# A decoder layer with its order and engines written in two tables: both tables drawn up anew

## The chip, the cores and the metric

One core of a Trainium2 chip runs the whole layer. The metric is the device time of one execution in microseconds (us); several runs of the same kernel give a median. The profile is of one further execution, taken by the hardware profiler. Engines are named as in the profile: PE (TensorE, matrix multiply) with PEld (its weight loads), DVE (VectorE), ACT (ScalarE), POOL (GpSimd), SP (SyncE, which issues nearly all transfers).

## What is computed

The reference is one layer of a hybrid decoder with 512 tokens and model width 1024, all in float32. Cut to what matters:

```python
def reference(x, c, ...):                       # x (1, 512, 1024), c (1, 1024)
    mod = silu(c) @ ada_w + ada_b               # 6 vectors of 1024: shift, scale, gate, twice
    sh1, sc1, g1, sh2, sc2, g2 = split(mod, 6)
    h = rms_norm(x, pre_norm_mix) * (1 + sc1) + sh1
    y = hybrid_mixer(h, ...)
    x = x + (1 + g1) * rms_norm(y, post_norm_mix)
    h = rms_norm(x, pre_norm_mlp) * (1 + sc2) + sh2
    y = square(relu(h @ w_ff1)) @ w_ff2         # 1024 -> 4096 -> 1024
    return x + (1 + g2) * rms_norm(y, post_norm_mlp)

def hybrid_mixer(h, ...):
    g_rnn, x_rnn, q, k_c, v_c, k_s, v_s, k_w, v_w, gate_logits = split(h @ w_in, ...)
    rnn = gelu(g_rnn) * rg_lru(causal_conv4(x_rnn))     # gated linear recurrence, width 512
    att = nsa_attention(...)     # 8 heads of 64; compressed + selected + window keys, ALiBi
    return concat(rms_norm(rnn), rms_norm(att)) @ w_out
```

## The kernel before

**Precision.** PE takes float32 numbers as a rounded high part and a low part, so most products are three matmuls: `mm3` issues high x high, high x low and low x high. Every operand has therefore to be split: a copy to the high part (`clk.copy`, on ACT or DVE) and a subtraction for the low part (`either("tensor_sub", ...)`, on DVE or POOL).

**Stages.** (1) The four token tiles of x are loaded and normalised (`XN`), transposed (`TR`) and modulated; ada weights give the shift and scale columns (`SU`). A first wave of matmuls (`MW`) makes six 512-column products at once in six PSUM banks while the weight tiles a0 to a7 arrive. (2) `AW` takes the wave out of PSUM: q to the tiles Q, keys to K1 and K2, and k_c and v_c to the tile kk, from which eight additions make the blocks `blk` of the compression. (3) `PR` runs the other projections in the order of the list ORDER: c00 to c13 (compression), x0 to x3 (recurrence input), q0 and q1, v, the recurrence's gates, g0 to g3. Later it runs the output projection (weight tiles o000 to o111). `VW` is the recurrence: conv, gates, scan, gelu. (4) `AS` makes the attention scores and their exponentials for 16 units, takes 1/denominator (`den`) and scales the tiles `p` by it; `AV` transposes the tiles p (PSUM tag tp), splits them into two tiles `pt` and multiplies by V (PSUM tag pv); `FA` finishes a token tile. (5) `RS` is the residual and norm, `TH` the transposes for the feed-forward part, `UF` the first four slices of the up projection. (6) `UP` is the up projection, one slice f0 to f31 of 128 columns at a time; `DA` is a first pass of the down projection over combinations of two slices (tiles ft, fs); `DN` is the second pass and the end: squares, norm, gate, residual and eight output transfers. `WL` loads the weight tiles (ring raw of four, SP's queue), `WS` splits them into hi_ and lo_ tiles. `AD` and `G2` make the other ada vectors out of tiles ar.

PSUM has eight banks, two for each of the tags f, s, pv and tp; whoever wants the next bank of a tag waits until the one before the last is read out.

**What sets the order.** The Python code calls the operations in some order, but during the recording nothing is issued: `put` appends each operation as a node, with the engines that could run it. At the end `flush` issues all nodes in the order of the table `PLAN`: 4836 nodes, two characters each, read as a number in base 90 with the digits of `ALPHA`. Where an operation could run on more than one engine (the copies of `clk.copy`, the operations of `either`, the choices of `clk.choose`), the table `PLACE` has one letter for it, by stream and in the order of recording: a for ACT, d for DVE, p for POOL. Each engine runs its own operations in the order of the table and waits by semaphores for the operands and the banks. The costs that stand in `act_way`, `elem_way` and `mm` order the recording only; the tables are drawn up elsewhere, by a planner that works with durations of its own.

```python
(way,) = self.nodes[ALPHA.index(a) * len(ALPHA) + ALPHA.index(b)].ways
way[2]()
...
mine = PLACE.get(self.name, "")[k:k + 1] if PLACE is not None else "adp"
ways = [w for w in ways if w[0][0] in (usual if mine in ("", ".") else mine)]
```

In the profile nearly every operation carries the line of the helper that issued it: L396 matmul, L400 transpose, L407 ACT, L441 DVE or POOL, L483 transfers. The tiles' names tell the operations apart; numbers in the names are left out (`hi_f` is the high part of some f slice, `r` a tile of the ring r8, `h` one of the h tiles).

Of the kernel before, what the change touches and what calls it, by code (L numbers as in the profile page):

```python
# [15 lines left out]
P = 128  # L16
S = 512
D = 1024
# [77 lines left out]
    '2d372E2K2~2G3S2c2j2g2e2f382b2l2i333V3T2k39352r2h2n342/2m2q363W2*2p3X2%2o2-3*3!3U2,3x3#2<2]3c3Y2?2=3y3C3Z'
    '3I3$2:3a2{2@583d2^3O3F3D3z3b3%3e3h3&3J3n3+3P3(3L3i3o3,3R3)3t4#3k3/4H3?3u4%3:3q4F3{3@45463w3A473G3M484M2.'
    '3|3f4O494C3l3r4A3<4N4B3-4g3=4G4$4h4i4k4l4m4j4Q4^4&4n4P4+4o4,4-4]GY4(4.2+2>4~4S5L504)2;514*3]5K4/2[4_3~4{'
    '4d2_3^5Y3E413K3Q52425D3B5X5M4|4}59533H3j445E5h5A5B5C435F5H5G3N5g5J3p3v5O3g3m5I5N5S3;5$3[5P3s4b7%5T3.5R3>'
    '4a3_3}4J5Q5#5Z5U5V5a5b5i5j5k4I5-5W5l5m5d5n5o5p5q5,5r4X5s7&4V5t5u4K5e627)6;4c6-5v4L5w6<6.6/5x6=5y615z5f6d'  # L100
    '5!5%6>6e4W6f7>6N674U6_6M5c6:7(68696@6A7?6V6B6{6?6C4e4R6D5_6E5&4Z4T6g6F4Y6G6H6I6U5(5)6[6J6|7+6K4f6q6}6L7|'
    '6h6O5*6p6P6i5+6]6^816Q6~6R6j6y5.5/6S6x6T6W5:726k5{716l6X6m6n5;5<7a6Y5=5>6a5?7b5@5[6Z5]73706o7c5^5}5|6r5~'
    '6c607C636s7B646t7R6u656v6w6b667N746z6!7S7D6#6$6%8L7z757T6&7@7!766(7[7o7]7}6)7~80777*7#788279836*847A7s85'
    '7t7p6+7q86877M88897r8A8B7w7u8V8W7vGW8Z8C8D8X7x7E8b7^8K8d937F8Y947,8E7-977_7.GZ957G997H7y7I9&7/8e4E7J8j9('
    '7K8k9)7L9+7O8h8F9,7P8f6,8G8O8i9E8P8QGa987Q7U9A9F7V8R9I7W9K7X9J9G7Y8M8S7Z8g7$7d8T7:7e8c9:7fG@9H8^8_9L8{9;'
    '7g8a9<7h7i968U8|8l8}7j8~9MAO8mG]90919*929B7;8u8q8v7kAP9=AU8w9N8x7l8y8r8z8!8#9l8$G^8%8&8(8)8*8n8+G_7m9C8o'
    '8,8t8-G[9m8.9T7<8p9D8N9V7=8s8/9O8:8H8;8<8=AV8>8I9W9n8?9r9o9s9X8@9Y9Z9aAS8[9b9R9c9p9d9t9e9v9f9w9x9q9y9g9U'
    'A59z8J9h9!AQAW9#ARA67{9$9iA79%AE9SAvB.A88]7nApAF9-AGAHAq9u9.AXA9B/AwAI9/9>AT9?9@Ar9[At9]9j9^9PAAAJAgCbAB'
    'CcAY9_C9AxAK9{AD9|9}9~AZ9QCdAdAcCiA.CAA/AuA0AhAzA!CNCjCkHPA>CpCqAsA#AfA?CrA:AeA@AiC#A<A$C$A%ALC%AaAjAbAM'
    'C+A&C,COA1C-A=BDBEANC/AyBHB5C:BJC;A[BFC<A(A;AkBtBIA]A2BGACA)BKHQBLA*AlA3B6BuB1BMA+B2BRB3C=A^BPC_A_BNC>A,'  # L110
# [1699 lines left out]
```

## Time and profile before

| | |
|---|---|
| median of three runs | 629.02 us (627.72 to 629.98) |
| the profiled execution, its own time | 627.82 us |
| its span, first to last instruction | 626.0 us, 9043 instructions |
| PE busy | 596.3 us (95%), 3060 matmuls and transposes |
| DVE busy | 539.2 us (86%) |
| ACT busy | 346.1 us (55%) |
| POOL busy | 209.1 us (33%) |
| moved by DMA | 102.15 MB, mean 163 GB/s |
| chain that ended last | PE 73%, DVE 11%, DMA 6%, ACT 5%, issue 3% |

A busy PE is not PE at its peak, since matmuls overlap; where matmuls follow one another without a wait, PE counts as busy throughout. A number in brackets behind a row of the timeline is the time for which the engine had been idle before it, and after the arrow stands what released it. The kernel's stages run one into the other: the wave ends at about 64 us, attention and recurrence lie between 98 and 269, the feed-forward part from 276 on.

### The profile page before, as it was taken

To read this page: it belongs to the slowest core of one execution; us is meant where nothing else is said; L and a number is where in the kernel's file an instruction comes from. 1 tells how busy PE (TensorE), PEld (TensorE's weight loads), DVE (VectorE), ACT (ScalarE), POOL (GpSimd) and SP (SyncE) were. 2 spreads that over 40 slices of the span, in tenths; PEclk is the share of its full clock that TensorE was granted. 3 is DMA by queue.
4 is the path that set the end of the run, shared out by engine and by line. 5 is a ranking of instruction groups with operands and counts; after the bars stand their busy time and mean duration, and the time that the engine had idled before them with its cause. 6 is when DMAs were issued, how large, how long until landed. Compare 5 with 4: busy or idle time off the path is not lost.

```text
span 626.0 us, 9043 instructions
## 1 busy us (share of the span) xinstructions
PE 596.3 (95%) x3060; PEld 497.9 (80%) x3060; DVE 539.2 (86%) x1072; ACT 346.1 (55%) x696; POOL 209.1 (33%) x209
## 2 busy tenths in 40 slices
PE   7999999998999999989999999999999999999992
PEld 6888788966777898869887888888887888878881
DVE  5986988979999988988888968787688789999897
ACT  6654525698999999687251220322322247465563
POOL 5001301652663175453204547641351231000113
PEclk9999999999999999999999999999999999999997
DMA  8968895430503302015664334254544426756613
GB/s 351 416 250 318 320 299 191 131 136 1 202 2 129 141 2 102 1 35 176 229 222 168 115 133 137 101 169 157 180 135 147 155 69 204 238 179 202 198 56 134
DMA packets 29430, 102.15 MB, mean 163 GB/s; under 512 B 3268, under 2 KB 3524, under 8 KB 29384
## 3 DMA queue, kind: packets, MB, share of 16 engines
q1 hardware_dynamic: 29240, 101.50, 46.4%
q8 instruction: 24, 0.39, 0.3%
q14 instruction: 22, 0.18, 0.1%
q10 hardware_dynamic: 144, 0.07, 0.0%
HBM read 99.47 MB, written 2.10 MB: 162 GB/s over the span
## 4 chain that ended last, share of the span: by engine, by line
PE 73%; DVE 11%; DMA 6%; ACT 5%; issue 3%; DVEq 0%; SPq 0%; ACTq 0%
PE f L396 36%; PE s L396 14%; PE pv L396 13%; PE tp L396 7%; DMA ar<-in_ada_t 4%; PE tp L400 4%; DVE r L441 3%; ACT p L407 2%; DVE fT L441 2%; ACT r L407 2%; DVE ar L441 1%; DMA raw_A11l<-in_wd 1%; DMA raw_A10l<-in_wd 1%; DVE p L441 1%; DMA r<-in_x 1%
## 5 line engine op out<-in xcount | busy, mean ns | idle before, releaser
L396 PE MATMUL f<-h,hi_f 128*128 128x512 f32 x224 | 87.7, 392 | 0.0
L396 PE MATMUL f<-h,lo_f 128*128 128x512 f32 x224 | 87.2, 389 | 0.0
L396 PE MATMUL f<-h2l,hi_f 128*128 128x512 f32 x224 | 87.2, 389 | 0.0
L407 ACT ACTIVATE fT<-f 128x512 f32<-128x512 f32 x30 | 17.8, 594 | 71.2 <-PE f L396 71.2
L396 PEld LDWEIGHTS f<-h,hi_f 128*128 128x128 f32 x224 | 42.1, 188 | 8.8 <-issue 0.2
L396 PEld LDWEIGHTS f<-h2l,hi_f 128*128 128x128 f32 x224 | 42.0, 188 | 8.6
L396 PEld LDWEIGHTS f<-h,lo_f 128*128 128x128 f32 x224 | 42.0, 188 | 8.5
L396 PE MATMUL f<-hi_o,h 128*128 128x512 f32 x128 | 47.7, 414 | 0.0
L407 ACT ACTIVATE p<-p,mx 128x32 f32<-128x32 f32 (+4 forms) x96 | 45.1, 472 | 3.8 <-DVE mx L441 3.6
L441 DVE TENSOR_TENSOR lo_f<-raw_f,hi_f 128x1024 fp32r<-128x1024 f32 x29 | 40.1, 1383 | 6.9 <-ACT hi_f L407 6.6
L400 PE MATMUL tp<-ident,p 128*128 128x128 f32 x192 | 41.6, 273 | 1.9 <-DVE pt L441 0.9
L396 PE MATMUL pv<-pt,V 128*128 128x256 f32 x160 | 42.2, 316 | 1.1 <-ACT pt L407 0.7
L441 POOL TENSOR_SCALAR p<-p,den 128x32 f32<-128x32 f32 (+4 forms) x43 | 35.7, 863 | 18.5 <-DVE den L441 15.5
L396 PE MATMUL s<-K,Q 128*128 128x288 f32 (+4 forms) x128 | 38.4, 336 | 0.5 <-DVE Q L441 0.3
L441 DVE TENSOR_TENSOR pt<-tp,pt 128x512 fp32r<-128x512 f32 (+1 forms) x56 | 33.6, 609 | 3.3 <-ACT pt L407 1.9
L407 ACT ACTIVATE hi_f<-raw_f 128x1024 fp32r<-128x1024 f32 x24 | 24.9, 1056 | 18.7 <-PE f L396 13.0
L396 PEld LDWEIGHTS pv<-pt,V 128*128 128x128 f32 x160 | 27.8, 189 | 6.1 <-DVE pt L441 2.1
L396 PE MATMUL s<-r,fs 128*128 128x512 f32 x96 | 32.5, 389 | 0.0
L396 PE MATMUL pv<-r,fs 128*128 128x512 f32 x96 | 31.8, 391 | 0.4 <-DVE r L441 0.4
L400 PEld LDWEIGHTS tp<-ident,p 128*128 128x128 f32 x192 | 25.0, 140 | 7.8 <-issue 1.8
L396 PE MATMUL tp<-r,fs 128*128 128x512 f32 x96 | 30.6, 389 | 0.0
L441 DVE CUSTOM_DVE_ANT_0 ar<-ar,silb 128x1024 f32<-128x1024 f32 x16 | 21.6, 1352 | 6.4 <-DMA ar<-in_ada_t 6.4
(732 smaller groups left out, 1817.0 us busy)
## 6 DMA issues: line engine op xcount, KB each, us to landing
raw_f<-in_wf SPq DMA_DIRECT2D x32, 512.0 KB, 3.5
...
```

The source lines that it names most:

```text
L396: lambda: self.nc.tensor.matmul(out, lhs, rhs, start=start, stop=stop))
L400: self.issue("pe", 0.109, [out], [src], lambda: self.nc.tensor.transpose(out, src, ident))
L407: return "act", cost, lambda: self.nc.scalar.activation(out, src, func, scale=scale, bias=bias, **kw), func
L441: return eng, cost, lambda: fn(out, *args, **kw), None
```

## The change

The operations, their operands and their dependences stay as they are. Both tables are replaced: `PLAN`, the order of all 4836 operations, and `PLACE`, the engine of those that have a choice. The planner was run with corrected durations for evacuations (reading PSUM out), transfers and GpSimd. The order of the streams and of the items in ORDER is untouched, and so are tile sizes, buffer counts and semaphores' rules.

```diff
 PLACE = {
-    '': 'dd',
...
-    'AV': 'dadaadddddaddddaaddadaaaaaaaaadaaaadaaaadaaaadaaaadaaaad',
-    'AW': 'adadaaddpppddpdp',
...
-    'TH': 'daddaadpddddaadddddddappddpddadd',
-    'UP': 'ddddddpdpddddpddpdddddddpddddddd',
-    'VW': 'pppdddpddppdppppppp',
...
-    'XN': 'aaaaaadaaaaa',
+    '': 'ad',
...
+    'AV': 'adddadddddaddddaaadadaaaaaaaaadadaadaaaadadaaaaaaadaaaad',
+    'AW': 'adaaaaaapdppdddd',
...
+    'TH': 'daddaaddddddaadddddpdaddadpdaadd',
+    'UP': 'ddpdddpddpddddddddpppdddddpddddd',
+    'VW': 'pdpdddpddppdppppppp',
...
+    'XN': 'paadaaaddaaa',
 }
 
 PLAN = (
-    '000O0P020Q0106400R0S0T0U0V0M074p4q084r0a0W0y040b4sGX4t090c030&0d0X0A554u0C4v054w0e4x0(0-4y0Y0H0N4z4!0D4:'
...
+    '000O0P020Q030R010S4E400T0U0V074p4q08090a0y0W0A0M0H0C0z0&0I0X0N0J0b4r0-4s0c0Y0B0(4t4u0D0)4v4w0d4x4y0=4z0Z'
...
 )
```

In PLACE 206 letters differ; the streams not shown with changes are AS (scalings of p and small products), DA, DN, FA and WS.

More of the change, by code (lines that the diff above doesn't have):

```diff
@@ L96 @@
[L96 to L110, printed above, removed]
@@ L181 @@
[L181 to L183 removed]
+    '000O0P020Q030R010S4E400T0U0V074p4q08090a0y0W0A0M0H0C0z0&0I0X0N0J0b4r0-4s0c0Y0B0(4t4u0D0)4v4w0d4x4y0=4z0Z'
+    '0E0.0*0e4!0!4:4;0f4<554=0>060^4>0/4?0F4@4[0g0G0h4D0i0;0_0:540?0|0{0}0j1O0#0~0K0kGX0]0L101E110l560@1P1C0m'
@@ new lines @@
+    '0+0n1F0o0[121j140,130p160%0q1k1G15181v170r19041l1H1A0s571B1D0<0t1J0u1M1=0v1I0w1N0x1K1R1Q1X1V1m0$1L1b1n1T'
+    '1U1>1o1]1p1q1W1r1a1s1^051S1w1c1_1t1{1Z1Y1?1e2M1x1|1h1g1@1$201z1[1i1u1f2X2Q1!2N2L1)1+1}1(1.1d1#2Y2&1;2R1y'
+    '2721242S2x1*1%2s1:222y1/2O2T1,2V2P262C1~2Z2z1&2U1-2v2(1<28232D2t30292J2F252a2u2w2|312I2)2B2H2E32332W2!2A'
+    '2$2G2}2c2e2#2K2g2m372k2~2%2f3V2i352o3S2l2r3c2/3W2*3T2b342h3X2?2,2{363!2<2n3d2]2q2d2j382p2-3*3F2:3U2@3y39'
+    '3#3$3%3e3Y3C3a3I3A3x2=3Z2^3L3D3O3z3b3h3&3J3P3+3R3(3k3i3n3t3)3,3/3?4#3o4F3u3{4%3G453:GY3q473w4H3M3@3|462.'
@@ new lines @@
+    '4A3<2+3f4M482;2>4B4O494$4g4C2_3l3r4h4N4k4^3-4Q4l4i4m4]3=4j4&3]3E4P4n2[4o4(3K5L4+4)4,4-5K4*3B4.3~4/4_584S'
+    '4b4{5Y4|4~4}503H5M59513^523N41535D5X5E4c5F3Q5G425A3j5h3p445B3g5C433v5H5J3;3m5g3s5O3.3>3_5I5S7%5N5$5P3[7&'
+    '4a3}5T5Q5R4J5Z5a4d5b5i5V5#5j5k5l5m7(5n7)4W5W5o5-5p5q5d5U5r5s5,5t5u4V5v5w4I6d5x4R625y4U5z5e4L5c6-4X6;6.4K'
+    '5!6<6e6=4Y6/6>67685%616_6{5&6f6g696M6N6:6A6B5(5)7+4G4e6V6C6@5f6D7>6[6?6|4Z6E6F6G4T5*6H6}6h6U6I6]6J6i6j7?'
+    '5+6q6K5.4f5/6^5:6p6~5;5_6L6O726k6P6y5{6Q6R5<6S6T7|5|6W5=6X6x5>6l5?7a6Y5@8173716Z6m5[7b6a5]6n6o5^706r766s'
@@ new lines @@
+    '6t5}6c5~7C60776u6b63646v7B7R74656w75666z8L7S787o6!6#7@7z796$7M7A7[6%6&7N7]7p6(7}7~GW7q806)827s7!837D7t84'
+    '6*7r7u7w857v7#86877x887^896+8A7,8d8V8B7_8W7-8X7E8Z7.8b8a8e7F8h93948C7G977H997I8j957J8f7$7K8g9E9&988D9F8K'
+    '9(8k7L8E9A7O7P8c7/9I8FGZ9+7Q7;968G6,7y7U8Y7V7c8O8i8P9)8Q9K7T7W9G8R7X9:9L9;8S7Y7:7Z8T7d9,8U7eGa7f9J8^7g9H'
+    '7hG@7iAO8_7j9M8{G[8|G]8}8~7{90918u9N8l927<8v8w8m8x7k9B8s8yAP8r7=8q8z9<8!8#9C7*8$8n9=9S8%9O8&9D8(8p9V7l8)'
+    '9R8*9W8o9X8+8t8M9l9Q8,G^9r9m8-8.8/7m8:8;8<9YAU8=8H8>9n9o8?9Z9a9*8I9bAV8@9s9cAQ9dAS8[9e9p9f9v9t9wApAW9x9g'
@@ new lines @@
+    '9y9q9z9h9!A5ATAv9#9uAE9$AR8N9%9U9-9TAF9.AqB.9/8]9i9PA6AG9>AtAH9?A7ArA87n9jAXAwA9AA9@CbAuAIB/9[9]AKAB9^AY'
+    'CcAxCdAZA.AJAy9_9{AgA>C9CiADCj9|9}A?ALAcAdCk9~CACpA0AzA!CNA#CqAhA/AfAiCrAeA:A<C#AsC$A@A$AjACC%A%AbC+HPBL'
+    'A;BDC,A1C-A&COAaC/A[B1BEC:BFC;A=BJBMBHC<AMBKB2B5BtA2ANA3BIA(BGB3A4A)A]CPA*BuC=BRA+G_B6BNAkA^C>BPCBA|B4A,'
+    'AlBvB:B78JA~A-A}B9B,BwHQAmBAC_B-C1B8A{B0CWAoBnBhC3C2HRCVBiBoBBBjC4BkBpHSCHCXA_BlCQBCBcCICJAnBmCUBqCLCRCK'
+    'BrBdCSBxCMB#ByC@BsB$CZBzC{B%C[C|DVC~C]D0CTD1D2CeD3ChD4D6CaD7CoD8D9CYDADWDBDCCuDDDEB!CfB(DXDFDG9kDHCmDIDJ'
@@ new lines @@
+    'CwCzDKB)B*DLClDMC)C^C!DOBeDPDQCvDNDRD$CnCtD%DSD+DTFhD@C&D[DUD]CsDYC*DZDaDbC?D,DuD^DcDdDhD_CxDiDvBSD{C(Dw'
+    'DjD!BQDkD)B+B&B;BOD|DyD#DlBTD&DmCgD(B<E6C}DzD}DnDxDoDpD*DqDeECCyDrD~E0D-BUDsD.BbBVBaDtDfBYEsBWEtFjB@BZEu'
+    'C.E1B[EvB]B^E2E3EwD5D=E7B|B=EDExB_E*E+E8BXD?E4EAGUE,FlE9E[EEB}EaE]B{EgEbE^BgFnE_EeEBE{E|BfFAEFB?EhFBD/Ec'
+    'FCHEF%FIFJB>D:C5EfE5EiD>E-FKEdB~FdEjHFFeFfE=E.FgEGC6D;EHFkC0EkE>D<C7EIE?C8EJElEWE/EQE;EKCCFRErFSEpEXEoCD'
+    'ELEYFoEqFLFMFTEMF|ENEZEOFPCEEnEPF}F~G,F&ERESH>HNETF4FNG-EUF5F<F,FiH?G0F-G3EyF6F=EVFmG4F>E}HKE~EzF0F:G.F7'
@@ L184 @@
+    'r3q:rSr4rTq;rUrVrkrPrXrlrmrnrWrorpr5r1rYr8rarqrZr9rcrrrsrdq=rur6rerbr7q<rfrwrvq>rxrgryrirhrzrtrjr!r$r#r%'
 )
```

162 lines of the change are left out of this document (75 added, 87 removed).

## The prediction

> **What bounds the kernel now.** I read the page's head first, then the stretches (busy time of each engine by stage), then PE in order of time for every place where it stood idle, with what ended the wait in brackets, and last the groups of ACT, DVE and POOL by shape for the prices of the moved operations. In the stretches the columns are PE, PEld, DVE, ACT and POOL busy, granted clock, DMA share and GB/s.
>
> ```profile
> span 626.0 us, 9043 instructions
> ...
> 0.00:20.00 20.00, 15.32 (x107) 14.95 (x108) 13.18 (x48) 14.32 (x27) 8.80 (x21) 1.00 0.92 365
> 20.00:100.00 80.00, 76.89 (x420) 64.12 (x419) 68.78 (x116) 37.96 (x58) 6.91 (x7) 1.00 0.84 308
> 100.00:150.00 50.00, 47.41 (x268) 37.83 (x269) 43.41 (x134) 42.25 (x112) 22.45 (x20) 1.00 0.34 116
> 150.00:200.00 50.00, 46.34 (x250) 37.34 (x248) 48.47 (x150) 47.50 (x127) 27.79 (x29) 1.00 0.24 86
> 200.00:250.00 50.00, 50.00 (x323) 43.71 (x321) 45.94 (x146) 46.47 (x117) 22.91 (x29) 1.00 0.27 95
> 250.00:300.00 50.00, 47.22 (x313) 42.46 (x312) 43.97 (x73) 36.42 (x65) 21.25 (x30) 0.97 0.24 79
> 300.00:515.00 215.00, 214.60 (x964) 177.02 (x963) 173.18 (x264) 59.89 (x101) 84.65 (x64) 1.00 0.45 151
> 515.00:570.00 55.00, 54.48 (x239) 44.48 (x238) 52.57 (x72) 31.74 (x44) 3.90 (x3) 1.00 0.61 199
> 570.00:626.00 56.00, 44.04 (x195) 35.99 (x193) 49.70 (x77) 29.55 (x51) 10.40 (x6) 0.93 0.42 143
> sum 626.00, PE 596.29 PEld 497.90 DVE 539.21 ACT 346.10 POOL 209.07; mean PE 66.25 PEld 55.32 DVE 59.91 ACT 38.46 POOL 23.23
> ```
>
> PE is the bound. From 300 to 515 it idles 0.40 us and issues a matmul every 214.60 / 964 = 0.22 us: nothing can be won there, only lost. PE is idle 29.71 us in all (626.00 - 596.29): 4.68 in the first 20 us and 11.96 after 570, mostly an end in which DVE works alone, which leaves 13.07 us in waits between. That is the ceiling for an order that does the same matmuls. From 100 to 250 ACT and DVE are nearly as full as PE, so their queues decide there. These are the waits that I weigh, PE's own rows:
>
> ```profile
> 49.69 0.43 PE L396 MATMUL s<-r,raw_c 128*128 128x64 f32 x2 [0.83 <-POOL r L441]
> ...
> 69.54 0.66 PE L396 MATMUL s<-r,raw_c 128*128 128x64 f32 x4 [0.69 <-DMA raw_c<-in_wc]
> ...
> 73.30 0.47 PE L396 MATMUL f<-h,hi_x 128*128 128x512 f32 x1 [0.76 <-DVE Q L441]
> ...
> 94.10 0.40 PE L396 MATMUL f<-lo_v,h 128*128 128x280 f32 x1 [0.44 <-DVE lo_v L441]
> ...
> 147.59 0.50 PE L396 MATMUL f<-h,hi_g 128*128 128x512 f32 x1 [1.91 <-ACT r L407]
> 148.55 0.53 PE L396 MATMUL s<-K,Q 128*128 128x288 f32 x2 [0.34 <-DVE Q L441]
> 159.05 0.73 PE L396 MATMUL f<-h,hi_g 128*128 128x512 f32 x2 [1.03 <-ACT r L407]
> 173.16 0.41 PE L400 MATMUL tp<-ident,p 128*128 128x128 f32 x2 [0.88 <-DVE pt L441]
> 182.34 0.50 PE L396 MATMUL pv<-pt,V 128*128 128x256 f32 x2 [0.24 <-DVE pt L441]
> 192.78 0.39 PE L396 MATMUL pv<-pt,V 128*128 128x256 f32 x1 [0.69 <-ACT pt L407]
> 276.05 0.39 PE L396 MATMUL pv<-h,hi_f 128*128 128x256 f32 x1 [1.08 <-ACT hi_f L407]
> 278.08 0.39 PE L396 MATMUL pv<-h,lo_f 128*128 128x256 f32 x1 [1.41 <-DVE lo_f L441]
> ...
> 482.67 0.50 PE L396 MATMUL pv<-r,fs 128*128 128x512 f32 x1 [0.40 <-DVE r L441]
> 554.25 0.50 PE L396 MATMUL f<-hi_B5b,fs 128*128 128x512 f32 x1 [0.53 <-DVE fs L441]
> ```
>
> **The change part by part.** Nothing is added or removed. Two characters of PLAN number one of 4836 recorded operations, one letter of PLACE gives an engine, so both orders can be written out. 206 operations change engine: 65 from POOL to DVE, 43 from DVE to POOL, 43 from DVE to ACT, 38 from ACT to DVE, 9 from POOL to ACT, 8 from ACT to POOL. The stages keep their places: on PE each projection ends within some 1.7 us of matmuls of where it ended. So I price place by place, with these rows:
>
> ```profile
> 47.52 1.21 ACT L407 ACTIVATE r<-s 64x512 f32<-64x512 f32 x2 [0.75 <-DVE r L441]
> 48.15 1.31 DVE L441 COPY r<-s 64x511 f32<-64x511 f32 x2 [0.66 <-ACT r L407]
> 53.98 0.57 DVE L441 TENSOR_TENSOR r<-r,vecs 128x248 f32<-128x248 f32 x1
> 146.94 0.60 ACT L407 ACTIVATE r<-f 128x512 f32<-128x512 f32 x1
> 276.81 1.21 DVE L441 TENSOR_TENSOR lo_f<-raw_f,hi_f 128x1024 fp32r<-128x1024 f32 x1
> 551.27 2.32 DVE L441 TENSOR_TENSOR lo_B5b<-raw_B5u,hi_B5b 128x1024 fp32r<-128x1024 f32 x1
> 551.16 1.36 POOL L441 TENSOR_TENSOR fs<-fT,fs 128x512 fp32r<-128x512 f32 x1 [21.59 <-ACT fs L407]
> 611.04 1.32 DVE L441 TENSOR_TENSOR stat<-stat 128x1 f32<-128x1 f32 x2
> 616.85 0.15 DVE L441 TENSOR_TENSOR stat<-stat 128x1 f32<-128x1 f32 x1
> L441 POOL TENSOR_SCALAR p<-p,den 128x512 f32<-128x512 f32 x7 | 10.9, 1568 | 0.4 <-DVE mx L441 0.4
> L441 POOL TENSOR_SCALAR p<-p,den 128x256 f32<-128x256 f32 x6 | 6.8, 1130 | 2.8 <-DVE mx L441 2.2 <-DVE den L441 0.7
> L441 POOL TENSOR_SCALAR p<-p,den 128x384 f32<-128x384 f32 x3 | 3.9, 1316 | 1.4 <-DVE den L441 1.4
> L407 ACT ACTIVATE p<-p,den 128x512 f32<-128x512 f32 x6 | 4.2, 716 | 1.2 <-DVE den L441 1.2
> L407 ACT ACTIVATE p<-p,den 128x256 f32<-128x256 f32 x6 | 3.0, 501 | 0.7 <-DVE den L441 0.7
> L441 DVE TENSOR_SCALAR p<-p,den 128x384 f32<-128x384 f32 x6 | 2.7, 476 | 0.0
> ```
>
> *Opening.* Seven of the eight kk evacuations go to ACT. The one that the second blk add of c00 needs was the first of DVE's pair and ended at 48.15 + 0.69 = 48.84; now it is third in ACT's run from 47.52, at 0.60 each: 49.3. PE has no more work ahead of c00 than before, so +0.4 (0 to +0.6). The first 30 loads keep their order.
>
> *Projections.* Ahead of c10 (69.54) PE now has one x0 and some x3 matmuls more, 1.5 us, over its wait of 0.69: -0.69. Later loads change places by two or three behind it; if c10 lands later, 0. Ahead of x2 (73.30) stand 0.84 us more, but DVE has a blk add (0.57) put in front of the Q evacuation that frees the bank: 0.76 + 0.57 - 0.84 = 0.49 is left, -0.26 (0 to -0.76). lo_v (94.10) has 0.3 us less ahead of it on DVE: -0.3 (0 to -0.44).
>
> *Recurrence.* At 147.59 ACT runs the same Q, Q, g0 evacuations and g2 still follows q1; two pv matmuls now stand between: -0.24 (0 to -1.91). At 148.55 the scores follow three g2 matmuls where they followed one and a pv: -0.34. At 159.05 g2's last matmul now directly precedes g3's first, which takes a bank of the same two-deep ring: at best the 0.60 evacuation and some 0.16 of handing over; I leave the 1.03 (0, -0.27 to +1). New is the same pattern before the first o000 matmul, directly behind g1's last: +0.76 (0 to +1.91).
>
> *Attention.* Before 173.16 two o000 matmuls (0.45) are put in and DVE's pt has 0.9 us less ahead: -0.88 (0 to -0.88). Before 192.78 a pv, a score, an o001 and a score are put behind the transposes, 0.6 us: -0.6. The pv group of 182 comes 0.85 us behind its release, where evacuation, subtraction and handing over take 1.47: 0.6 for 0.24, +0.4 (0 to +0.7).
>
> *First up projection.* At 276.05 and 278.08 both queues have the same work ahead of hi_f and lo_f: 0 (0 to -2.49). If RS or TH were faster upstream, hi_f (ACT) is next late.
>
> *Feed-forward, 300 to 570.* 80 of the changes are moves between POOL and DVE in DA, UP and WS; DVE is 173.18 of 215 busy and POOL 84.65. At the old durations of the same shapes the largest shift within 50 us is some 4 us onto DVE and 13.6 off POOL, so PE stays the cover: 0. Were that cover gone, one late operand costs what 482.67 and 554.25 cost, 0.4 to 0.5. 482.67 has 1.1 us more PE work ahead: -0.40. 554.25 hangs on lo_B5b, which took 2.32 for the usual 1.21 while POOL ran the subtraction at 551.16; that one goes to DVE (some 0.7 there): -0.5 (0 to -0.53).
>
> *End.* PE is idle for most of its 11.96 us here because DVE is still at work. DVE's two stat adds at 611.04 take 1.32, where one alone takes 0.15; they run beside a POOL subtraction. The new order has the first of them two operations earlier. -0.8 (0 to -1.1). The Trainium skill, SBUF — State Buffer, Who interferes with whom, says that a VectorE instruction with two SBUF inputs and a GpSimd instruction that reads SBUF exclude each other, the later one waiting for the whole of the earlier. By that rule lo_B5b would start at 551.16 + 1.36 = 552.52 and end at 553.73; the trace has 553.59, so it agrees. By that rule the end would win the whole 1.1 and the sum would be 0.3 us better. The same rule speaks against the 51 operations newly on POOL, each of which can hold a DVE subtraction.
>
> Sum: gains 0.69 + 0.26 + 0.30 + 0.24 + 0.34 + 0.88 + 0.60 + 0.40 + 0.50 + 0.80 = 5.01; losses 0.40 + 0.76 + 0.40 = 1.56; net -3.45 us. The profiled execution took 627.82 us (span 626.0 and 1.82 around it) and would take 624.4. The median of the three runs, 629.02, is 1.20 above it; carried over, **625.6 us**.
>
> **The rivals.** *Slower: late POOL copies.* Between 195 and 221 us five scalings of p go to POOL: three of 128x256 (1.130 for 0.501 on ACT), one of 128x512 (1.568 for 0.716), one of 128x384 (1.316 for 0.476 on DVE): 1.89 + 0.85 + 0.84 = 3.58 us. The transposes read these tiles. It decides where the transposes stand closer behind the scaling than POOL's time, about 1.1 to 1.6 us. If so, the waits move there and the gains of recurrence and attention (2.06) are not seen either: -3.45 + 3.58 + 2.06 = +2.2, 631.2 us. Against it: 200 to 250 has PE at 50.00 of 50. For it: the stage's ACT and DVE are over 45 of 50 busy.
>
> *No change: waits wander.* All gains sit where a two-deep bank ring or an in-order queue hands over; removing one exposes the next, as g3 and o000 show. The losses of 1.56 and others like them eat the gains: 629.0, within 1.9 us. For it: ACT gets about 2 us more between 150 and 200, where it is busy 47.50.
>
> *Larger gain.* The new order also clears 276.05, 278.08, 159.05 and 49.69: 2.49 + 1.03 + 0.83 = 4.35 more and no new loss: 629.02 - 5.01 - 4.35 = 619.7. Against it: the queues ahead of these four are the same.
>
> **How the numbers follow.** Forecast (gain of 2 to 7 us) 0.49, larger gain 0.08, no change 0.26, slower 0.16. A measurement of this kernel can tell about 0.3%, 1.9 us, from no change. So faster 0.57, same 0.26, slower 0.17. The range goes from just below the larger gain, 619.5, to the slower rival with most of the g3 term's upper end, 632.0, and leaves out some 0.07 on each side; the likeliest case alone spans 622 to 627.
>
> **What would show it.** PE idle between 20 and 570 falls from 13.07 to about 10.5; the rows for c10, x2, tp at 173 and pv at 192 lose their brackets; 147.59, g3 and the first hi_f and lo_f keep theirs; a new one of about 0.8 stands before the first o000; lo_B5b takes 1.21; DVE's last stretch ends a microsecond nearer to PE's last matmul. 300 to 515 stays at 214.6. The forecast is wrong if transposes between 195 and 225 show brackets with POOL p, or if 300 to 515 loses PE time.

## The result, and the profile after

The new tables are slower by 0.6%: 632.91 us median against 629.59 for the old ones run beside them, a ratio of 1.0062 (95% interval 1.0044 to 1.0081). The forecast was 625.6 us with a range that ended at 632.0. The profiled execution took 632.88 us, its span 5.1 us more than before's 626.0.

The stretches of the changed kernel, cut as in the prediction (PE, PEld, DVE, ACT and POOL busy, granted clock, DMA share, GB/s), under the page's head:

```profile
span 631.1 us, 9049 instructions
...
20.00:100.00 80.00, 76.97 (x423) 64.47 (x421) 67.90 (x108) 39.64 (x61) 6.78 (x6) 1.00 0.85 305
100.00:150.00 50.00, 46.09 (x258) 36.62 (x257) 45.35 (x138) 38.61 (x108) 18.50 (x19) 1.00 0.37 127
150.00:200.00 50.00, 45.54 (x240) 36.64 (x241) 47.16 (x149) 48.23 (x123) 27.77 (x25) 1.00 0.27 96
200.00:250.00 50.00, 49.79 (x317) 42.97 (x316) 46.29 (x143) 44.41 (x118) 23.68 (x28) 1.00 0.23 75
250.00:300.00 50.00, 46.98 (x312) 41.07 (x311) 43.64 (x82) 40.81 (x78) 17.25 (x28) 1.00 0.23 80
300.00:515.00 215.00, 214.09 (x970) 176.73 (x969) 169.87 (x274) 59.63 (x102) 62.04 (x53) 1.00 0.46 153
515.00:570.00 55.00, 54.31 (x238) 44.05 (x237) 51.55 (x73) 32.64 (x45) 3.02 (x2) 1.00 0.59 190
570.00:631.10 61.10, 48.21 (x213) 39.63 (x211) 54.81 (x83) 30.36 (x51) 6.97 (x5) 0.92 0.41 139
```

Between 20 and 570 us PE stands idle for 550 - 533.77 = 16.23 us, where it stood for 13.07; the forecast was 10.5. It now issues 258 matmuls between 100 and 150, ten fewer than before, so a loss arises ahead of 150. 200 to 250 is nearly as full as it was (49.79 for 50.00), and 300 to 515 lost half a microsecond.

PE's own rows that have a wait in the changed kernel (start, time, the wait ahead of it in brackets):

```profile
50.24 0.43 PE L396 MATMUL s<-r,raw_c 128*128 128x64 f32 x2 [0.73 <-POOL r L441]
...
73.41 0.47 PE L396 MATMUL f<-h,hi_x 128*128 128x512 f32 x1 [1.06 <-DVE Q L441]
...
94.27 0.40 PE L396 MATMUL f<-lo_v,h 128*128 128x280 f32 x1 [1.25 <-DVE lo_v L441]
...
102.09 0.51 PE L396 MATMUL s<-K,Q 128*128 128x288 f32 x2 [1.10 <-DVE mx L441]
...
123.20 0.38 PE L396 MATMUL s<-K,Q 128*128 128x256 f32 x1 [0.75 <-DVE mx L441]
...
150.00 0.74 PE L396 MATMUL f<-h,hi_g 128*128 128x512 f32 x2 [1.72 <-ACT r L407]
151.23 0.53 PE L396 MATMUL s<-K,Q 128*128 128x288 f32 x2 [0.27 <-DVE Q L441]
...
161.28 0.74 PE L396 MATMUL f<-h,hi_g 128*128 128x512 f32 x2 [0.80 <-ACT r L407]
...
175.60 0.50 PE L396 MATMUL f<-hi_o,h 128*128 128x512 f32 x1 [0.56 <-ACT r L407]
...
178.42 0.41 PE L400 MATMUL tp<-ident,p 128*128 128x128 f32 x2 [0.56 <-DVE pt L441]
...
195.72 0.39 PE L396 MATMUL pv<-pt,V 128*128 128x256 f32 x1 [0.16 <-ACT pt L407]
...
279.96 0.39 PE L396 MATMUL pv<-h,hi_f 128*128 128x256 f32 x1 [1.06 <-ACT hi_f L407]
281.33 0.39 PE L396 MATMUL pv<-h,lo_f 128*128 128x256 f32 x1 [0.75 <-DVE lo_f L441]
...
499.40 0.50 PE L396 MATMUL pv<-r,fs 128*128 128x512 f32 x1 [0.64 <-DVE r L441]
...
534.29 0.50 PE L396 MATMUL pv<-hi_B0b,fs 128*128 128x512 f32 x1 [0.36 <-DVE ar L441]
```

The c10 wait of 0.69 is gone; x2 waits 0.3 longer; lo_v waits 1.25 for 0.44; the waits at 102 and 123 us stand where the prediction had nothing. No row between 195 and 225 has a bracket with POOL p.

What a new wait costs can't be read off its bracket alone, because both kernels wait at other places too. So both traces were laid side by side by **PE's work done**: at the moment when the same sum of matmul work is finished, how far is the new order behind the old one? The steps of this lag are the losses by place. The second column is a further execution of the same new order, against the same old trace.

| stretch, us of the old trace | what lies there | lag grows by | second execution |
|---|---|---|---|
| 0 to 63 | opening | +0.22 | +0.38 |
| 63 to 92 | c10, x2 | -0.88 | -0.89 |
| 92 to 120 | lo_v, first scores | +1.97 | +0.03 |
| 120 to 130 | den, accT (below) | +1.57 | +1.58 |
| 130 to 154 | g2, scores, g3 | -0.41 | -0.40 |
| 154 to 252 | attention, o000 | +1.35 | +1.42 |
| 252 to 288 | first f slices | -1.00 | -0.98 |
| 288 to 319 | up projection begins | +0.85 | +1.35 |
| 319 to 479 | | -0.09 | +0.36 |
| 479 to 485 | r8 at 482 | -0.69 | -0.69 |
| 485 to 520 | r8 at 499 | +0.94 | +0.94 |
| 520 to 535 | second pass begins | +1.28 | +1.39 |
| 535 to 556 | lo_B5b | -0.83 | -0.84 |
| 556 to end | norm, gate, output | +0.80 | +0.89 |

Most steps repeat to a few hundredths; 288 to 319 and 319 to 479 differ by half a microsecond each. The stretch that differs most, 92 to 120, is one in which PE waits behind a tile that is still landing.

DVE's and POOL's rows of the changed kernel at the places with a loss:

```profile
91.96 1.23 DVE L441 CUSTOM_DVE_ANT_0 ar<-ar,silb 128x1024 f32<-128x1024 f32 x1 [0.65 <-DMA ar<-in_ada_t]
93.19 1.03 DVE L441 TENSOR_TENSOR lo_v<-raw_v,hi_v 128x840 fp32r<-128x840 f32 x1
...
95.95 1.23 DVE L441 CUSTOM_DVE_ANT_0 ar<-ar,silb 128x1024 f32<-128x1024 f32 x1 [1.27 <-DMA ar<-in_ada_t]
97.56 3.86 DVE L441 SCALAR_TENSOR_TENSOR r<-r,vecs,r 128x512 f32<-128x512 f32 x4
98.79 1.42 POOL L441 TENSOR_TENSOR lo_v<-raw_v,hi_v 128x560 fp32r<-128x560 f32 x1 [28.46 <-ACT hi_v L407]
...
120.14 2.65 POOL L441 TENSOR_TENSOR lo_q<-raw_q,hi_q 128x1024 fp32r<-128x1024 f32 x1 [1.53 <-ACT eg L407]
121.05 1.76 DVE L441 TENSOR_TENSOR den<-sm,eg 128x6 f32<-128x6 f32 x1
...
126.44 2.40 POOL L441 TENSOR_TENSOR lo_g<-raw_g,hi_g 128x1024 fp32r<-128x1024 f32 x1 [1.69 <-ACT hi_g L407]
127.38 2.00 DVE L441 SCALAR_TENSOR_TENSOR accT<-ar,sil,accT 128x512 f32<-128x512 f32 x1
...
497.44 1.36 POOL L441 TENSOR_TENSOR raw_A13u<-raw_A13u 128x512 f32<-128x512 f32 x1 [11.26 <-DVE r L441]
497.57 1.78 DVE L441 TENSOR_TENSOR r<-raw_A12l,r 128x512 fp32r<-128x512 f32 x1
...
614.88 2.90 POOL L441 TENSOR_TENSOR ar<-ar,fT 128x512 f32<-128x512 f32 x2 [0.84 <-ACT fT L407]
615.51 0.92 DVE L441 TENSOR_TENSOR stat<-stat 128x1 f32<-128x1 f32 x1 [0.18 <-ACT junk L407]
616.79 1.53 DVE L441 SCALAR_TENSOR_TENSOR fT<-fT,stat,r 128x512 f32<-128x512 f32 x1
```

And the same four operations about 120 us in the kernel before:

```profile
118.56 2.41 POOL L441 TENSOR_TENSOR lo_q<-raw_q,hi_q 128x1024 fp32r<-128x1024 f32 x1 [1.74 <-ACT hi_q L407]
120.19 0.81 DVE L441 TENSOR_TENSOR den<-sm,eg 128x6 f32<-128x6 f32 x1
...
123.31 0.89 DVE L441 SCALAR_TENSOR_TENSOR accT<-ar,sil,accT 128x512 f32<-128x512 f32 x1
124.74 2.42 POOL L441 TENSOR_TENSOR lo_g<-raw_g,hi_g 128x1024 fp32r<-128x1024 f32 x1
```

An addition of 128x6 numbers took 1.76 us: it started at 121.05, while POOL's subtraction had 1.74 us to run, and ended 0.02 after it. Not one of these operations changed engine at 120 and 127 us. What changed is when the POOL instruction starts: in the old order DVE's addition met only its last 0.78 us, and the accT product-sum started before POOL did.

### The profile page after: what moved, and what is told of

It reads as the page before. It is cut to its first block, busy times and chain, and to the rows that moved or that the text cites. A ratio compares the mean times of both kernels' runs of the same rounds, so it can differ in the third digit from the quotient of the medians.

```text
span 631.1 us, 9049 instructions
## 1 busy us (share of the span) xinstructions
PE 596.8 (95%) x3060; PEld 496.5 (79%) x3060; DVE 539.6 (86%) x1089; ACT 347.8 (55%) x702; POOL 175.5 (28%) x186
## 4 chain that ended last, share of the span: by engine, by line
PE 76%; DVE 12%; ACT 6%; DMA 4%; issue 1%; DVEq 0%; POOL 0%; ACTq 0%
PE f L396 38%; PE s L396 15%; PE pv L396 12%; PE tp L396 7%; PE tp L400 4%; DVE r L441 3%; DMA ar<-in_ada_t 3%; DVE fT L441 2%; DVE ar L441 2%; ACT r L407 1%; DVE p L441 1%; ACT h L407 1%; DMA vecs<-in_vecs 1%; DMA raw_B0l<-in_wd 1%; DVE Q L441 1%
## 5 line engine op out<-in xcount | busy, mean ns | idle before, releaser
L441 DVE TENSOR_TENSOR lo_f<-raw_f,hi_f 128x1024 fp32r<-128x1024 f32 x31 | 41.5, 1341 | 1.3 <-ACT hi_f L407 1.1
L396 PEld LDWEIGHTS s<-K,Q 128*128 128x128 f32 x128 | 23.0, 189 | 6.2 <-issue 1.4
```

The lines of the kernel that those rows point to most:

```text
L396: lambda: self.nc.tensor.matmul(out, lhs, rhs, start=start, stop=stop))
L441: return eng, cost, lambda: fn(out, *args, **kw), None
```

## The experiments

Each ratio is to the old order, run in turn on the same chip, with a 95% interval. In the diffs a line is one operation in the order of issue, with its engine; only operations that move are shown, with the one that they come to stand behind or ahead of. "Lag" is the one of the table above, against the first old trace.

**Which part of the order.** The first 1040 operations of the order reach to some 131 us. One kernel takes these from the old tables and the rest from the new, the other is its mirror; the new order ran beside them.

```diff
 old_until_131: PLAN, PLACE
-first 1040 operations: new
+first 1040 operations: old (the others: new)
 new_until_131: PLAN, PLACE
-first 1040 operations: old
+first 1040 operations: new (the others: old)
```

> The changed kernel once more, unaltered, as the yardstick for the other three and for a second trace. By matmul work done, the first trace of the new order falls behind the old one in steps: about +0.7 us at lo_v (94 us), +0.9 at the scores that wait for the maxima (102), +0.9 at the scores at 123, +1.0 between 125 and 131, +0.8 at 499, +1.3 at 530, -0.8 at 555, +0.9 in the end. If these steps belong to the order, the second trace has them at the same places, within 0.3 us each, and the ratio to the kernel before is again 1.006 (+3.3 to +4 us). If they are scatter from execution to execution, the steps stand at other places and the ratio comes out anywhere from 1.003 to 1.009.

> The first 1040 operations in the old order on the old engines (PE's work to about 131 us), all others in the new order on the new engines. Theory A, the loss sits in a few places between 92 and 131 us: this kernel takes back 2.9 of the 3.5 us, ratio to the kernel before about 1.001 to 1.002, that is some +1 us from 230 to 560 us and the end. Theory B, the loss is spread over the whole order and every stage pays a part: it takes back about a fifth, ratio 1.005.

> The mirror: the new order and engines up to about 131 us of PE's work, the old ones for the rest. Theory A: +2.9 us, ratio about 1.0046. Theory B: under +1 us, ratio at most 1.0015.

Measured: the new order 632.7 us, 1.0074 (1.0046 to 1.0101); old until 131 us 628.08, 1.0000 (0.9973 to 1.0027); new until 131 us 630.96, 1.0053 (1.0031 to 1.0074). The first fifth of the time holds most of the loss, 3.3 us by this ratio (1.9 to 4.6), and the four fifths behind it cost nothing that can be measured, within 1.7 us either way.

**The two operations held by POOL.** `after_apart` is the new order with POOL's and DVE's work about 125 us pulled apart, and two conv steps moved behind the evacuation for which the scores wait; these are five operations, none on another engine. `before_collide` puts the meetings of about 125 us into the old order.

```diff
 after_apart (new order)
+ACT hi_q1, POOL lo_q1      behind the next attention evacuation
-ACT hi_q1, POOL lo_q1      ahead of it
+DVE accT product-sum       behind the next split of pt
+DVE two conv steps         behind the next score evacuation
 before_collide (old order)
+ACT hi_q1, POOL lo_q1      two ACT operations later
+DVE accT product-sum       behind the next score evacuation
```

> The new order with seven of its 4836 operations moved by some places, no engine changed: the split of q1 (ACT's copy and POOL's subtraction) behind the next evacuation, so that POOL's 2.65 us no longer cover DVE's den at 121; one accT product-sum behind the evacuations at 130, so that POOL's subtraction for g1 no longer holds it (2.00 us for 0.74) in front of them; two conv steps of DVE (one of them held by POOL for 1.88 us in place of 0.75) behind the three maxima at 102 for which the scores wait. Theory A, these three POOL instructions that hold DVE's two-operand instructions cost PE 0.9 + 0.9 + 0.8 us: the lag at 135 us falls from 2.8 to about 0.3, the time by about 2.5 us against the changed kernel run beside it, ratio to the kernel before about 1.002. Theory B, a wait that is removed turns up behind the next operand: the waits at 102, 123 and 130 go, but the lag at 135 us stays above 2 us and the time falls by less than 0.8 us. Theory C, the late ada tile in front of lo_v (94 us) is the root and all later waits follow from it: the wait at 94 stays 1.2 and so does most of the loss, less than 1 us is won.

> The kernel before with two of the collisions put in by moving three of its operations a few places: the split of q1 behind the next exponential, so that POOL's subtraction starts just ahead of DVE's den, and one accT product-sum behind a score evacuation, so that POOL's subtraction for g1 holds it. Work and engines are the same. Theory A: den at 120 takes 1.4 to 1.8 us for 0.81, the product-sum about 2.0 for 0.88, PE falls behind by 0.6 + 0.6 = 1.2 us between 120 and 131, and the time is 1.2 us longer, ratio 1.002 (1.001 to 1.003). Theory B: DVE has slack there, PE's lag at 135 us is under 0.3 us, ratio 1.000.

Three rows of after_apart's timeline:

```profile
95.77 0.40 PE L396 MATMUL f<-lo_v,h 128*128 128x280 f32 x1 [2.08 <-DVE lo_v L441]
...
123.14 0.16 DVE L441 TENSOR_TENSOR den<-sm,eg 128x6 f32<-128x6 f32 x1
...
124.16 2.40 POOL L441 TENSOR_TENSOR lo_q<-raw_q,hi_q 128x1024 fp32r<-128x1024 f32 x1 [3.45 <-ACT hi_q L407]
```

and before_collide's:

```profile
117.93 2.41 POOL L441 TENSOR_TENSOR lo_q<-raw_q,hi_q 128x1024 fp32r<-128x1024 f32 x1 [2.33 <-ACT eg L407]
118.92 1.44 DVE L441 TENSOR_TENSOR den<-sm,eg 128x6 f32<-128x6 f32 x1
...
124.11 2.39 POOL L441 TENSOR_TENSOR lo_g<-raw_g,hi_g 128x1024 fp32r<-128x1024 f32 x1
124.28 2.76 DVE L441 SCALAR_TENSOR_TENSOR accT<-ar,sil,accT 128x512 f32<-128x512 f32 x1
```

Apart, the same addition takes 0.16 and the lag between 120 and 130 us grows by 0.07, where it grew by 1.57. Put together in the old order, the two take 1.44 and 2.76, and the lag there grows by 2.49. As times: after_apart 631.25, 1.0044 (1.0023 to 1.0065); before_collide 630.51, 1.0039 (1.0019 to 1.0059). So the two meetings alone make the old order some 2.5 us slower (1.2 to 3.7 by the interval), twice what was expected. Taking them out of the new order leaves a loss; its trace has the lo_v wait at 2.08, a granted clock of 0.61 from 96 to 100 us behind it, and a lag of +3.65 between 92 and 120 us.

**The waits at 94 and 102 us.** Ahead of lo_v DVE runs a product on an ada tile. In the new order that tile is asked for at 87.17 us (before: 85.94): SP waits until an earlier product frees a buffer, and that product is late because DVE waits 1.18 us, until 84.11, for hi_x, whose x1 tile was moved behind c12 and two ada tiles. c13's 0.5 MB, too, now go ahead of it. At 95.95 the next such product waits 1.27 us for its tile, five conv steps stand behind it, of which POOL's lo_v holds some (3.86 us for four steps), and only then comes the maximum for which PE waits at 102 us.

```diff
 after_ada (new order)
+SP load x1           ahead of the load of c12
+SP load c12, c13     each behind the ada tile that it stood ahead of
 after_late_ada (new order)
+DVE ada product      (the one at 95.95 us) behind the next score evacuation
 after_front (new order)
+after_late_ada, after_apart's first two moves, after_ada's x1 and c12
 after_lov
+after_front, and DVE lo_v ahead of the ada product at 91.96 us
```

> The new order with three transfers put back to where the old order had them: the weights x1 in front of c12, c12 behind the next ada tile, and c13 behind the ada tile that the new order lets it pass. No engine and no other operation is changed. Theory A: in the new order x1 lands late, DVE stands 1.2 us at 84 waiting for ACT's copy of x1 with the ada product behind it, the ada tiles after it are issued and land later, and DVE, in order, reaches lo_v late; PE's wait for lo_v at 94 (1.49, 0.91, 1.03 and 2.33 us in the four traces of this part of the new order, 0.63 and under 0.2 in the two of the old) falls below 0.6 and the time by about 0.9 us against the changed kernel; ratio to the kernel before 1.005 or 1.006. Theory B, the wait at 94 is scatter of the transfers: it stays near 1.4 on average and the time is the changed kernel's.

> The new order with one DVE instruction moved: the ada product that the new order put in front of five conv steps at 94 us (the old one had it behind them) goes behind the maxima of the first scores; the load into its buffer follows it. Theory A, in-order DVE waits there 0 to 1.9 us for a tile that lands at 93.8 to 96.7, and with the conv steps late, POOL's subtraction for v2 (98 to 100) holds one of them another 1.1: PE's wait for the maxima (scores at 102: 1.27, 0.2, 1.09 and 1.75 us in four traces) goes, DVE runs through from 94 to 98, and the time falls by 1 to 1.5 us against the changed kernel; ratio 1.004 to 1.005. Theory B, what decides is only the late tile in front of lo_v: the wait at 94 stays and so does the ratio, 1.006 to 1.007.

> The new order with three things put right in its first 131 us: that ada product; x1's weights loaded in front of c12 as in the old order; the split of q1 and the accT product-sum out of POOL's way. Theory A, these are all that the new order loses in its front: it comes to the kernel with the old front, which measured 1.000, that is ratio 1.000 to 1.002, and by work done its lag at 135 us is within 0.7 us of its lag at 75 us. Theory B, the front loses by many small things: ratio 1.003 or more and new waits of 0.5 us and more between 90 and 131 us.

> The kernel with the front of the new order put right in three places (1.0027), and DVE's low part lo_v in front of the ada product that waits for its tile, not behind it. Theory A, the rest of the front's loss is this wait: PE's wait at 94 us (1.64, 1.13 and 1.2 on average) falls under 0.3, 1.2 to 1.7 us are won, ratio 1.000 to 1.001, as with the old front. Theory B, the rest is spread: the wait goes but less than 0.5 us is won, ratio over 1.002.

| | median us | ratio | lag, 92 to 120 us | 120 to 130 us |
|---|---|---|---|---|
| new order, two executions | 632.91 and 632.7 | 1.0062 and 1.0074 | +1.97, +0.03 | +1.57, +1.58 |
| after_ada | 631.2 | 1.0054 (1.0035 to 1.0072) | +1.19 | +1.58 |
| after_late_ada | 631.77 | 1.0051 (1.0029 to 1.0074) | +0.42 | +1.57 |
| after_front | 630.12 | 1.0027 (1.0006 to 1.0049) | +0.95 | +0.05 |
| after_lov | 629.82 | 1.0035 (1.0019 to 1.0051) | -0.71 | +0.07 |

after_ada's rows on PE show what a mended load order met next:

```profile
92.33 0.43 PE L396 MATMUL s<-r,raw_c 128*128 128x64 f32 x2 [0.67 <-DMA raw_c<-in_wc]
...
101.26 0.50 PE L396 MATMUL s<-K,Q 128*128 128x288 f32 x2 [0.92 <-DVE mx L441]
```

The lo_v wait is gone and c13, now later, is waited for. Both moved loads count, by one trace each: in after_front, with x1 put back and c13 not, the ada tile is asked for at 86.42 and DVE still waits 1.22 for it; in after_ada, with c13 put back too, it is asked for at 86.41 and DVE waits 0.17. In after_late_ada the 102 us wait is gone (the four conv steps take 2.73) and lo_v keeps 0.88. Only after_lov, with all of it, has no wait of 0.3 us or more on PE between 80 and 120. Its time is not better than after_front's: 1.0035 and 1.0027 came from two chips, and their intervals overlap. By its trace its front is mended (at 130 us it is 1.4 us ahead of the first old trace), yet 1.0035 is left where the old front left 1.0000. These two intervals overlap as well, so how this rest divides between the front and what follows it stays open.

**All mends together.** `after_mended` joins after_ada, after_apart's first two moves, and three mends behind 480 us; `after_sum` joins after_lov with two of these.

```diff
 after_mended = after_ada + hi_q1, lo_q1, accT of after_apart
+DVE r8 subtraction (499 us)   ahead of the ft combination that stood before it
+DVE ar addition (534 us)      ahead of two fs combinations
+last 136 operations           old order (no engine differs among them)
 after_sum = after_lov
+DVE r8 subtraction (499 us)   as above
+last 136 operations           old order (no engine differs among them)
```

> The new order with all places mended that the traces show as losses that repeat, each by moving one to three operations: the three transfers above; the split of q1 and the accT product-sum out of POOL's way (121 and 127 us); the low part r8 that POOL holds at 497 three places earlier on DVE; the two ar sums at 530 in front of two fs subtractions, one of which POOL holds; and from 559 us of PE work on the old order and engines for the end. Theory A, the loss is the sum of these places: -1.5 - 0.9 - 0.9 - 0.7 - 0.9 = -4.9 us against the changed kernel, which leaves about 1 us below the kernel before, ratio 0.998 (0.996 to 1.001). Theory B, waits wander: each mended place sends its work to the next and less than half is won, ratio 1.004 or more.

> The same, and behind the front the two other losses of the new order that can be undone at their place: the low part r8 that POOL holds at 497 us three places earlier (-0.45), and the old order and engines for the end (-0.9). Theory A, the loss of the new order is the sum of its places and is then accounted for: ratio 0.998 to 0.9995, at or below the kernel before. Theory B, other losses remain: ratio over 1.001.

after_mended 630.55, 1.0038 (1.0015 to 1.0060): in its trace PE waits 1.59 at 102 us and 0.87 at 536 us, so the move at 534 us only shifted that wait. after_sum 627.90, 1.0007 (0.9991 to 1.0024), span 624.8: with the front mended, the r8 mend (lag 485 to 520 us +0.65, where after_lov has +1.48) and the old end (-0.01 for +0.88), the loss is no longer measurable. Against after_lov, run beside it, that is 1.9 us for two moves worth 1.7 by their traces. It is 1.2 with the step of the other new traces at 499 us, +0.94, in place of after_lov's.

**Can the new order's gains be kept?** Three kernels keep the old order from 75 to 131 us and take places where the new order gained; two move the recurrence's wait of 1.9 us.

```diff
 blend (old order)
+operations 0 to 540 and 140 operations about 280 us: new
+DVE r8 (482 us) earlier; the POOL partner of lo_B5b (551 us) on DVE; one end sum on DVE
 old_new_old
+first 1040: old; then new with r8 (499 us) earlier; last 136: old, one end sum on DVE
 old_new_old_g0 = old_new_old
+ACT g0 evacuation ahead of an in-place step of the recurrence; 10 g2 matmuls ahead of a score
 before_g0 (old order)
+ACT g0 evacuation as above; 12 g2 matmuls ahead of a score
```

> The kernel before with the pieces of the new order that its traces show as gains that repeat: the new order for the first 540 operations (to about 75 us: -0.9 at c10 and x2) and between about 269 and 288 us (the first lo_f: -0.65); and three single edits: one low part r8 four places earlier on DVE (482 us: -0.5), the subtraction beside lo_B5b on DVE instead of POOL (551 us: -0.8) and one sum of the end on DVE instead of POOL, which held a stat add for 1.1 us (611 us: -0.4). Theory A, each place counts by itself: -3.3 us, ratio 0.995 (0.993 to 0.997), and the kernel beats both. Theory B, waits wander: within 1 us of the kernel before, ratio over 0.998.

> The old order and engines up to 131 us and again from 559 us of PE work on, the new ones between, with the low part r8 that POOL holds at 497 us put three places earlier, and one sum of the end (611 us) on DVE instead of POOL. Against the kernel with the old front alone, which measured 1.000: -0.45 at 497, -0.9 for the old end, -0.5 for the sum of the end. Theory A, places that repeat add up: ratio 0.997 (0.995 to 0.999), faster than both kernels. Theory B: 1.000.

> The fastest kernel so far (old, new, old: 0.9981) with ACT's evacuation of the gate g0 moved from behind the two evacuations of q1 into a gap of ACT before them (its product is ready 5 us earlier), ten g2 matmuls in front of the two scores that wait for Q3, and the first B0 tile split ahead of the second. Theory A: PE's waits of 1.9 at 146 and 0.7 at 526 us go, and with the first the half clock that follows it in some executions (matmuls of 0.43 us in place of 0.23 for some 3.4 us): -1.9 - 0.7 and -0.7 on average, ratio 0.993 to 0.995. Theory B, the waits reappear one operand later: ratio 0.997 or more.

> The kernel before with only that evacuation and those matmuls moved (twelve, with the two that the old order has behind the scores). Theory A: the wait of 2.08 at 148 us goes in the trace, the granted clock stays 1.00 from 140 to 160 us in every trace, 2 to 3.4 us are won, ratio 0.995 to 0.997. Theory B, the wait moves to the scores or to g3: ratio over 0.999.

blend 627.53, 0.9994 (0.9972 to 1.0016); old_new_old 627.16, 0.9981 (0.9956 to 1.0005); old_new_old_g0 626.55, 0.9996 (0.9977 to 1.0014); before_g0 628.65, 1.0021 (0.9995 to 1.0046). blend's trace shows the gains one by one (482 us -0.69, lo_B5b -0.81, end -0.51) and beside them +4.40 between 92 and 120 and +2.72 between 520 and 528. The g2 wait did what the rival "waits wander" says; a row of PE in before_g0, and a stretch of it:

```profile
152.88 0.38 PE L396 MATMUL pv<-pt,VC 128*128 128x256 f32 x1 [2.04 <-DVE pt L441]
```

```profile
150.00:155.00 5.00, 2.96 (x13) 2.02 (x12) 5.00 (x16) 2.60 (x14) 1.32 (x1) 1.00 0.01 2
```

PE no longer waits 1.91 for the evacuation, and waits 2.04 for DVE five microseconds on. Between 150 and 155 us DVE is busy for 5.00 of 5: DVE bounds this stretch, and an earlier evacuation on ACT doesn't shorten it.

**How far one old execution stands for the others.** The old order was traced once more, and the place at which its traces differ most was taken by itself.

```diff
 before_b0 (old order)
-DVE subtraction on the first tile of the second pass (raw_B0u, from a landing load)
 DVE low part of A15l, which PE needs at 525 us
+DVE subtraction on raw_B0u
 old_best (old order)
+the move of before_b0; blend's edits without its operations 0 to 540
```

> The kernel before, unaltered, for a second trace. In the three traces that run the old order behind 131 us PE loses another 0 to 4 us at two places that lose nothing in the first trace: at 211 us (the ada sum waits for its tile) and at 527 us (a low part waits behind the B0 tiles). If these places depend on when a transfer lands, this trace has a loss there between 0 and 4 us, its order-bound waits (122, 148, 173, 276, 278 us) repeat to 0.1 us, and the first trace was a lucky one. If they belong to the experiments' edits, the loss is 0 in both places.

> The old order with one move: DVE's subtraction on the first tile of the second pass (raw_B0u, which waits for a transfer that has yet to land) goes behind the last low part of A15l, which PE needs at about 525 us. In five of six traces of the old order PE waits there for 0.8 to 2.2 us and falls behind by 1.8 to 4.2 us; in the profiled one it doesn't. Theory that this wait on a landing tile in DVE's queue costs the average execution some 2 us: PE's row at 525 has no bracket, the lag between 520 and 535 us is within 0.6 us of the profiled old execution, and the ratio is 0.997 (0.995 to 0.999). Rival, that PE meets the late tile anyway some matmuls on (the high part of B0): the bracket moves to the f matmul on hi_B0b or lo_B0b, ratio 1.000.

> The old order with that move, and with the places where the new order gained in every trace: the new order of 140 operations about the first f slice (-1.0 us), the r8 subtraction at 482 us (-0.7), the lo_B5b partner on DVE at 551 us (-0.8), one end sum on DVE (-0.5). If gains of this kind add up, -3.0 us by traces and about -2 more on average from the move at 525 us: 623 to 625 us, ratio 0.992 (0.990 to 0.995). Rival, that waits wander: 0.997 to 1.000, and the trace shows new brackets of 0.5 us or more behind the places that were mended.

before_again took 629.54 us, its span 627.8. Two stretches of it and one row of PE:

```profile
146.00:150.00 4.00, 2.99 (x9) 2.29 (x10) 3.60 (x7) 3.95 (x6) 1.33 (x2) 0.68 0.00 0
...
524.00:528.00 4.00, 2.74 (x7) 1.74 (x8) 4.00 (x6) 3.63 (x6) 0.00 (x0) 0.79 0.57 186
...
525.16 0.73 PE L396 MATMUL s<-r,fs 128*128 128x512 f32 x2 [1.57 <-DVE r L441]
```

It loses 1.4 us at about 150 and 3.6 us at 525, and at both places the granted clock falls (0.68 and 0.79 of the stretch, where the first old execution had 1.00 in both). Of six traces with the old order at 525 us, five wait there, 0.8 to 2.2 us, and fall behind by 1.8 to 4.2; the first one, from which the prediction's sum was made, doesn't. In the twelve traces with the new order there the step from 520 to 528 is -0.3 to +0.8. before_b0 shows that the tile, not DVE's order, is late:

```profile
522.08 0.69 DVE L441 TENSOR_TENSOR raw_B0u<-raw_B0u,raw_B0l 128x512 f32<-128x512 f32 x1 [0.68 <-DMA raw_B0l<-in_wd]
...
524.86 0.50 PE L396 MATMUL f<-hi_B0b,fs 128*128 128x512 f32 x1 [1.63 <-ACT hi_B0b L407]
```

The wait for r is gone, and PE waits for the tile's high part a few matmuls on: 629.90, 1.0019 (0.9995 to 1.0043), as its rival said. old_best 627.56, 0.9998 (0.9972 to 1.0024): its trace holds the four gains (-1.12, -0.69, -0.68, -0.51) and a span of 624.9, and the gain in the medians is not to be told from none. No version here beats the old order beyond its interval; old_new_old comes nearest.

## Why the prediction was wrong, step by step

**Right, against the first old trace.** c10 lost its wait: no trace of the new front has one there, and nine of the old front have 0.46 to 1.66. The stretch with c10 and x2 gained 0.88 (predicted 0.95), though not as told: x2 waits 1.06 rather than 0.49, and the part of the gain that the two brackets don't hold isn't assigned. In six of eight further traces of the old front PE goes through this stretch 0.3 to 0.7 us faster than in the first, so a part of the 0.88 belongs to that one execution. r8 at 482 gained 0.69 (0.40 predicted), lo_B5b 0.83 (0.50); but in six traces of the old order the first wait is anything from 0 to 0.40, and the second, 0 to 0.94, is missing in two of them without any change. g2, the scores and g3 together gained 0.41 against 0.58. At 192.78 the wait fell by 0.53 (0.60 predicted). The opening cost 0.22 and 0.38 (0.40), but eight further traces of the old front scatter there from -0.7 to +0.6 against the first, so this agreement can be luck.

**The step that failed first: "lo_v (94.10) has 0.3 us less ahead of it on DVE: -0.3".** It counted DVE's work and not what that work waits for. "Later loads change places by two or three behind it; if c10 lands later, 0" followed the moved loads to c10 only; x1, c12 and c13 moved as well. Through hi_x and the ada tile they made PE wait 1.25 for lo_v where it had waited 0.44. In the five traces with these loads and lo_v as the new order has them the wait is 0.67 to 2.08; in eight further traces of the old front it is 0. Every instruction of the moved loads had to be followed to the queue that waits for it.

**The step priced at nothing: DVE held by POOL.** The prediction quoted the rule and then left "the 51 operations newly on POOL, each of which can hold a DVE subtraction" at 0. The dear ones of the front were not even among these: lo_q, lo_g and lo_v ran on POOL in both orders, and the new times of their starts made them meet a DVE operation that the next score needs. 120 to 130 us cost 1.57, which removal and insertion both show; at 102 us a further part of the loss. At 499 us it is 0.93 (0.65 is left with the mend): there one of the 51, raw_A13u's subtraction of 1.36 on POOL, makes the r8 subtraction 1.78 for 0.68.

**"End: -0.8" was +0.88.** No engine differs among the last 136 operations; their order did it. One pair of POOL additions left the stat additions, another met two operations of the last chain: 0.92 for 0.15 and 1.53 for 0.75. With the old end the loss is gone in two traces (-0.00, -0.01).

**Attention and the o000 wait: net -0.32, measured +1.35 and +1.42.** The terms were 0.88 and 0.60 won, 0.76 and 0.40 lost. The wait at 173 fell by 0.32 rather than 0.88 (178.42), that at 192 by 0.53; the one predicted for o000 is there with 0.56 (175.60), and others of 0.6 to 0.7 came behind it. That is the rival "waits wander", at its place; no run divides this sum further.

**"Feed-forward: 0".** The cover of 300 to 515 held as a whole (PE idles 0.91 for 0.40), yet +0.9 and +1.4 near 318 us and +1.3 and +1.4 between 520 and 535 stand against it. The first is the matmul that sums accT, at 318.43: in all twelve traces with the new order there it starts 0.10 us behind the last of accT's product-sums on DVE, in the eight with the old order 1.42 to 1.45 behind. So PE now waits for product-sums that DVE takes up too late. Of the second, 1.0 is DVE held by POOL again:

```profile
529.94 2.38 DVE L441 TENSOR_TENSOR fs<-fT,fs 128x512 fp32r<-128x512 f32 x2
530.45 1.32 POOL L441 TENSOR_TENSOR raw_B1l<-raw_B1l,raw_B1u 128x512 f32<-128x512 f32 x1 [30.51 <-DMA raw_B1l<-in_wd]
```

These two combinations stand ahead of the ar addition for which PE waits at 534.29, and took 1.29 in the kernel before. Of the eleven traces that keep this order on DVE, ten have POOL start when its tile has landed. In four of the eleven it starts 0.4 to 0.5 us behind the first combination, ahead of the second, and DVE waits. In four others it starts 0.6 to 0.8 behind, the combinations take 1.29, and POOL's subtraction takes 1.64 to 1.86. In the last three they don't meet. after_mended, which moves the addition, has 3.21 for the two. hi_f and lo_f, put at 0, gained 1.0, about half of which the five other traces of the old order have too (0.43 to 0.50 faster there than the first).

**The base.** The sum started from one execution of the old order that happened to meet no landing tile at 525 us. There the new order is the better one on average by some 1.5 us, an estimate from the six and twelve traces: old +2.3 between 520 and 528, new +0.4, and new +0.5 more by 535. So traces of the new order show 2.2 and 3.4 us lost behind 131 us, where the medians of old_until_131 show none. In the front it was a slow execution: at 120 us eight further traces of the old front stand from 2.3 us ahead of it to 0.2 behind, 1.1 ahead on average. So the front's loss is larger than the first rows of the table say, as the ratio of new_until_131 has it.

**The rivals.** The result lies on the side of the slower rival (631.2) but not by its mechanism: transposes between 195 and 225 us wait for no POOL scaling. The chance of slower was worked out from that one mechanism alone and left out the ones that came.

**DVE beside POOL, counted.** Taken are DVE operations that started while POOL still had 0.15 us or more to run of a subtraction or another operation on two tiles; "held" are those that took at least 0.1 us over their usual time and ended no earlier than POOL did. In the twenty traces it is 759 of 939 additions, subtractions and products with two SBUF inputs, 45 of 63 product-sums, and none of 589 with a PSUM operand. Of the 180 that were not held, 101 ran under a POOL instruction that itself took over 2.7 us, such as a 128x256 combination of 7.34 us at 455.75 in the kernel before, where others of this size took mostly 0.7 to 1.2; there, as at 534 us, it seems to be POOL that waits. The Trainium skill, SBUF — State Buffer, Who interferes with whom, has a VectorE instruction with two SBUF inputs contend with a GpSimd instruction that reads SBUF, and says that issue order decides which one waits. The traces agree in four fifths of these cases, and at 534 us they show both orders; by that rule the prediction's own sum would have needed the start of each POOL instruction, not their number.
